# The spatial gate's second matrix in seven block products, with the fill share of VectorE raised from 0.85 to 0.88

## The chip, the cores and the metric

One NeuronCore of a Trainium2 chip runs the whole kernel. The metric is the device time of one execution in microseconds (us); lower is better.

## The reference, cut to what matters

One encoder layer over 512 positions of width 1024. A normalised input `xn` is projected to twelve column groups; four mixers work on them; each mixer's output is projected back, gated, and summed.

```python
xn = rms_norm(h, norm1_g[i])
proj = jnp.einsum('bsd,dk->bsk', xn, w_in[i])
(sg_u, sg_v, g_q, g_k, g_v, g_r, g_a, a_q, a_k, a_v, c_a, c_g) = jnp.split(proj, cuts, axis=-1)
y_a = spatial_gating(jax.nn.gelu(sg_u), jax.nn.gelu(sg_v), ...)   # u * (W_s layer_norm(v) + b)
...
for n, y in enumerate((y_a, y_b, y_c, y_d)):
    gate = jax.nn.sigmoid(jnp.einsum('bsd,de->bse', xn, w_gate[i, n]) + b_gate[i, n])
    merged = merged + gate * jnp.einsum('bsk,kd->bsd', y, w_branch[i, n])
```

`sg_u` is `xn` (512 x 1024) times a 1024 x 512 matrix. `y_d` is a causal depthwise convolution with 31 taps on 512 channels, followed by a layer norm.

## The kernel before, in words

**Three products for one.** Every fp32 factor is split into a high part (copied by ScalarE to a rounded type, `hi`) and a rest (VectorE: value minus `hi`, called `lo`). A product is hi*hi + hi*lo + lo*hi, so each 128-row block costs three matmuls on TensorE. The weights come from HBM in pieces of 128 x 1024 (512 KB): `load_piece` issues the transfer on SP's queue into a tile `raw` (four of them), `split_piece` makes `wh` and `wl` (five of each).

**Order of the work.** One Python loop writes the program: each `step` makes the weights of the next pieces ready (up to three pieces ahead), writes the matmuls, then `fill()`, then the step's own evacuation. Generators on a list `side` are advanced at the start and in the middle of a step and carry the small work of the mixers. Each engine executes its own instructions strictly in the order written.

**The taps.** The convolution's 31 x 4 multiply-adds (a tap: 128 x 512, VectorE, tiles `pad` and accumulators `u`) are a `filler`. `fill()` writes taps as long as the VectorE cost written so far is below `FILL` times the TensorE cost written so far; both are the kernel's own estimates. After the last tap `conv_norm` starts.

**The gates in seven products.** The gate matrices of mixers 1, 0 and 3 are done in halves (512 of 1024 columns; `(1, 0)` is the first half of mixer 1's). For each half, 2 x 2 blocks of input and weights are combined so that seven block products (`Q1` to `Q7`) do instead of eight. The sums of input blocks, `s1` to `s4`, are made once on VectorE (`combine`, and `last_sum` for `s4`, which overwrites a quarter of `xn` and so has to wait for the last product that reads the whole of `xn`). The sums of weight blocks are made by the transfers: a tile `grow` or `raw` gets one block by SP's queue and then one or more blocks by transfers that add, which only POOL's queue issues (`load_piece`, `accum_op`). `Q6` adds a block to the tile of `Q5`, and `Q4` one to that of `Q6`, so each of these transfers also waits for the split of the product before it.

**Around the change.** The order of this part is: mixer 2 with its gates (`branch(2)`), then `sg_v` in four pieces (four output banks at once; TensorE reads `lo` of a piece with its second matmul), then `sg_u` in four steps of 128 columns. Two of these stand ahead of the first half gate and two between its first products; the last one starts `sg_mix` (the 128 x 128 mixing on TensorE, then VectorE) and `last_sum`. For `sg_v` and for mixer 2's weights (`BY_DMA`) the rest `lo` is not made by VectorE: ScalarE writes minus `hi`, and an adding transfer on POOL's queue puts the weights on top. POOL's queue also computes the small powers for the norms.

Of the kernel before, what the change touches and what calls it, by code (L numbers as in the profile page):

```python
# [9 lines left out]
AF = mybir.ActivationFunctionType  # L10
# [3 lines left out]
S = 512  # L14
# [24 lines left out]
W_SLOTS = 5  # L39
LEAD = 3  # L40
RAW = 4
FILL = 0.85
WARM = 4
E_SLOTS = 26
PAD = 16
# [22 lines left out]

def gate_steps():

    out = []
    for i, e in enumerate(GATES + (None,)):
        for p in GATE_ORDER:
            if p in ("B0", "B1"):
                out.append((p, GATES[i - 1]) if i else ("S", 2 + int(p[1])))
            elif e is not None:
                out.append((p, e))
    return out


def layout():


    out = []
    loads = []
    at = {}

    def flush():
        for i in range(len(at.setdefault("done", [])), len(out)):
            at["done"].append(i)  # L90
            loads.append(((i,), out[i][-1], None))

    tok = lambda n: [("tok", "w_in", COL[n], 512, (2 * i, 2 * i + 1), 1024) for i in range(4)]
    ch = lambda n, m: ("ch", "w_in", COL[n] + 128 * m, 1024)
    out += tok("a_v")
    out += [("gka", i, 816 if i < 2 else 544) for i in range(3)]
    out += tok("g_v")
    for m in range(4):
        out += [ch("a_q", m), ch("a_k", m)]
    for m in range(4):  # L100
        out += [ch("c_g", m), ch("c_a", m)]
    out += [ch("g_q", m) for m in range(2)]
    out += [ch("g_r", m) for m in range(4)]

    def branch(n):
        for m in range(8):
            out.append(("gate", n, m, 1024))
            if m % 2 == 0:
                out.append(("br", n, m // 2, 1024))

    branch(2)
    out += tok("sg_v")
    out += [ch("sg_u", m) for m in range(2)]
    flush()
    last = {}
    blocks = {}
    for p, e in gate_steps():
        if p == "S":
            out.append(ch("sg_u", e))
            flush()  # L120
        elif p[0] == "B":
            if int(p[1]) % 2 == 0:
                out.append(("br", e[0], 2 * e[1] + int(p[1]) // 2, 1024))
                flush()
        else:
            if p == "Q5":
                for b in ("11", "12", "21", "22"):
                    blocks[b] = len(out)
                    out.append(("gblock", *e, int(b[0]) - 1, int(b[1]) - 1, 1024))
                    at["done"].append(blocks[b])  # L130
            old = GATE_ONTO.get(p)
            new = GATE_SUMS[p][len(GATE_SUMS[old]) if old else 0:]
            loads.append((tuple(blocks[b] for b in new), 1024, last[old] if old else None))
            last[p] = len(loads) - 1
    out += [("ch", "w_out", 128 * m, 1024) for m in range(8)]
    flush()
    ff1 = lambda g, m: ("ch", "w_ff1", 1024 * g + 128 * m, 1024)
    out += [ff1(0, m) for m in range(8)]
    flush()
    for g in range(4):  # L140
        blocks = {}
        for e in ("11", "12", "21", "22"):
            for h in range(2):
                blocks[e, h] = len(out)
                out.append(("ff2", g, int(e[0]) - 1, int(e[1]) - 1, h, 1024))
                at["done"].append(blocks[e, h])
        last = {}
        for e in ORDER if g < 3 else ORDER_LAST:
            if e[0] == "F":
                out.append(ff1(g + 1, int(e[1])))  # L150
                flush()
            elif e[0] == "U":
                out.append(("tok", "w_ple", 512 * int(e[1]), 512, (0, 1), 1024))
                flush()
            else:
                for h in range(2):
                    old = ONTO.get(e) if g < 3 or e != "Q5" else None
                    new = SUMS[e][len(SUMS[old]) if old else 0:]
                    loads.append((tuple(blocks[n, h] for n in new), 1024, last[old, h] if old else None))
                    last[e, h] = len(loads) - 1  # L160
    for half in range(2):
        out += [("tok", "w_ple_gate", 512 * half, 512, (2 * i, 2 * i + 1), 1024) for i in (2, 3, 0, 1)]
    flush()
    return out, loads
# [9 lines left out]
def build(tc, x, w, vec, wa2, sgw, rows, rb, pt, out):  # L174
# [17 lines left out]
    def U(dt=F32):  # L192
        return epool.tile([128, 512], dt, tag="u", bufs=E_SLOTS, name=name("u"))
# [153 lines left out]
    def start(g, wait=0, first=False):  # L347
        side.insert(0 if first else len(side), [g, wait, "start"])
# [125 lines left out]
    base = {}  # L474
    j = 0
    for key, n in (("a_v", 4), ("gka", 3), ("g_v", 4), ("qk", 8), ("conv", 8), ("g_q", 2), ("g_r", 4), ("br2", 12),
                   ("sg_v", 4), ("sg_u", 2)):
        base[key] = j
        j += n
    for p, e in gate_steps():  # L480
# [525 lines left out]
    def last_sum():  # L1006

        for f in range(4):
            copy(quarter(1, 0, 0, f), x4[f // 2][:, 256 * (f % 2):256 * (f % 2) + 256])
        yield "mid"  # L1010
        for f in range(4):
            tt(quarter(1, 0, 1, f), x4[f // 2][:, 256 * (f % 2):256 * (f % 2) + 256],
               quarter(1, 0, 0, f).bitcast(F32), OP.subtract)
        xsum["s4"] = [[quarter(1, 0, q, f) for q in range(2)] for f in range(4)]
# [49 lines left out]

    start(sg_bias(), 0)
    tok_steps("sg_v", 4, xn, 512, after)
    def sg_u(m, j):
        def evac(b):
            t = U()
            ACT.activation(t, b, AF.Gelu_apprx_tanh)  # L1070
            su.append(t)
            if m == 3:
                start(sg_mix(), 0)
                start(last_sum(), 0, True)

        step(j, lambda b: ch_mm(b, j, xn), evac)

    for m in range(2):
        sg_u(m, base["sg_u"] + m)
    for n, i, k in (("a11", 0, 0), ("a12", 0, 1), ("a22", 1, 1)):  # L1080
        xsum[n] = [[quarter(i, k, q, f) for q in range(2)] for f in range(4)]
    xr = []
# [14 lines left out]
    def gate_product(p, e):  # L1097
        j = base[p, e]
        n, u = e
        bk = {"Q1": 2, "Q6": 2, "Q7": 2, "Q4": 2, "Q5": 3, "Q3": 3, "Q2": 1}[p]  # L1100
        fresh = p in ("Q1", "Q2", "Q5")

        def mms(_):
            if fresh:
                gb[bk] = bank()
            b = gb[bk]
            xs = xsum[gsum[p]]
            hi, lo = parts[j]
            seq = [(hi, f, q, m) for f in range(4) for m in range(2) for q in range(2)]
            seq += [(lo, f, 0, m) for f in range(4) for m in range(2)]  # L1110
            for i, (t, f, q, m) in enumerate(seq):
                if i == len(seq) // 2:
                    middle()
                mm(b[:, 256 * m:256 * m + 256], t[:, 256 * f + 128 * m:256 * f + 128 * m + 128], xs[f][q],
                   fresh and i == 0, i == len(seq) - 1, skip_group_check=True)

        def evac(_):
            b = gb[bk]
            b2 = b.rearrange("p (m t) -> p m t", m=2)
            if p == "Q1":  # L1120
                ga[e] = mpool.tile([128, 2, 512], F32, tag="ga", bufs=2, name=name("ga"))
                copy(ga[e][:, :, 0:256], b2)
            elif p == "Q5":
                gc[e] = mpool.tile([128, 2, 512], F32, tag="gb", bufs=1, name=name("gb"))
                copy(gc[e][:, :, 256:512], b2)
            elif p == "Q6":
                copy(gc[e][:, :, 0:256], b2)
            elif p == "Q2":
                o = ga[e][:, :, 0:256]
                tt(o, o, b2, OP.add)  # L1130
                for m in range(2):
                    gate_tanh(o[:, m], o[:, m], n, 4 * u + m)
            elif p == "Q3":
                o = gc[e][:, :, 0:256]
                tt(o, b2, o, OP.subtract)
            elif p == "Q7":
                o = gc[e][:, :, 256:512]
                tt(o, o, b2, OP.subtract)
                for m in range(2):
                    gate_tanh(gc[e][:, m], gc[e][:, m], n, 4 * u + 2 + m)  # L1140
            elif p == "Q4":
                for m in range(2):
                    gate_tanh(ga[e][:, m, 256:512], b2[:, m], n, 4 * u + m)

        step(j, mms, evac, own=False)

# [7 lines left out]
             lambda b: merge(4 * u + m, th, b, last=n == 3))  # L1154

    for p, e in gate_steps():
        if p == "S":
            sg_u(e, base[p, e])
        elif p[0] == "B":
            branch_product(int(p[1]), e)  # L1160
            if p == "B3" and e == (0, 1):
                start(load_residual(), 4)
        else:
            gate_product(p, e)
# [449 lines left out]
```

## Time and profile before

| | |
|---|---|
| three timed runs | 986.45, 989.26, 989.85 us, median 989.26 |
| the profiled execution's own time | 988.05 us |
| its span, first to last instruction | 986.3 us |
| TensorE busy | 967.6 us, 98% of the span |
| VectorE, ScalarE, POOL busy | 684.9, 457.7, 98.5 us |
| TensorE's mean granted clock | 0.996 |

The profiled execution took 1.75 us more than its span. A row of a timeline gives the start of an instruction (or of several merged ones, with their count after x), how long it took, the engine, the source line, what it writes and reads, and in brackets the idle time of the engine ahead of it with what ended it. Matmuls overlap, so their spacing (from one row's start to the next row's) is their cost, not their length.

### The profile page before, as it was taken

To read this page: it belongs to the slowest core of one execution; us is meant where nothing else is said; L and a number is where in the kernel's file an instruction comes from. 1 tells how busy PE (TensorE), PEld (TensorE's weight loads), DVE (VectorE), ACT (ScalarE), POOL (GpSimd) and SP (SyncE) were. 2 spreads that over 40 slices of the span, in tenths; PEclk is the share of its full clock that TensorE was granted. 3 is DMA by queue.
4 is the path that set the end of the run, shared out by engine and by line. 5 is a ranking of instruction groups with operands and counts; after the bars stand their busy time and mean duration, and the time that the engine had idled before them with its cause. 6 is when DMAs were issued, how large, how long until landed. Compare 5 with 4: busy or idle time off the path is not lost.

```text
span 986.3 us, 12889 instructions
## 1 busy us (share of the span) xinstructions
PE 967.6 (98%) x4990; PEld 821.3 (83%) x4990; DVE 684.9 (69%) x993; ACT 457.7 (46%) x685; POOL 98.5 (10%) x119
## 2 busy tenths in 40 slices
PE   8999999999999999999999999999999999999995
PEld 6978888887888899998998888888888888887885
DVE  6645897477899887877666553566576577578656
ACT  6473774235363435455454334434343345335633
POOL 5001000002121201110110000010001002011000
PEclk9999999999999999999999999999999999999998
DMA  6344332247598538765974233366468267667402
GB/s 231 119 129 128 118 84 78 86 113 186 110 242 226 142 104 223 179 162 143 249 220 129 86 118 117 87 147 171 129 171 209 72 190 183 198 176 187 132 22 86
DMA packets 43225, 144.96 MB, mean 147 GB/s; under 512 B 4859, under 2 KB 5276, under 8 KB 43164
## 3 DMA queue, kind: packets, MB, share of 16 engines
q1 hardware_dynamic: 32156, 104.29, 31.4%
q0 software_dynamic: 11008, 39.85, 21.9%
q8 instruction: 39, 0.64, 0.3%
q14 instruction: 22, 0.18, 0.1%
HBM read 139.92 MB, written 2.10 MB: 144 GB/s over the span
## 4 chain that ended last, share of the span: by engine, by line
PE 87%; DVE 7%; ACT 3%; issue 2%; DMA 1%; POOL 0%; SPq 0%; POOLq 0%; ACTq 0%; DVEq 0%
PE b L236 85%; DVE wl L218 2%; PE b L240 2%; DVE u L218 1%; ACT wh L231 1%; DVE u L222 1%; DVE ht L218 1%; DMA raw<-w 0%; DMA stack<-stack 0%; ACT u L231 0%; DVE s L218 0%; DVE gb L218 0%; ACT combo L231 0%; DVE ga L222 0%; DVE ht L222 0%
## 5 line engine op out<-in xcount | busy, mean ns | idle before, releaser
L236 PE MATMUL b<-x,wh 128*128 128x512 f32 (+1 forms) x1440 | 315.6, 363 | 1.7 <-DVE gb L218 1.7
L236 PEld LDWEIGHTS b<-x,wh 128*128 128x128 f32 x1440 | 244.0, 189 | 43.4 <-issue 3.7
L218 DVE TENSOR_TENSOR wl<-raw,wh 128x1024 fp32r<-128x1024 f32 (+2 forms) x150 | 182.2, 1223 | 75.8 <-ACT wh L231 74.4
L231 ACT ACTIVATE wh<-raw 128x1024 fp32r<-128x1024 f32 (+2 forms) x166 | 169.5, 1039 | 27.3 <-DMA raw<-w 18.9
L236 PE MATMUL b<-x,wl 128*128 128x512 f32 (+1 forms) x720 | 168.2, 361 | 0.0
L236 PE MATMUL b<-wh,combo 128*128 128x512 f32 x448 | 141.7, 390 | 0.6 <-DVE ht L218 0.6
L236 PEld LDWEIGHTS b<-x,wl 128*128 128x128 f32 x720 | 123.9, 189 | 20.7
L236 PEld LDWEIGHTS b<-wh,combo 128*128 128x128 f32 x448 | 84.1, 188 | 18.4 <-issue 0.9
L1234 ACT ACTIVATE act<-act 128x512 f32<-128x512 f32 x32 | 20.2, 632 | 147.8 <-DVE act L222 147.8
L236 PE MATMUL b<-wl,combo 128*128 128x512 f32 x224 | 87.5, 391 | 0.9 <-DVE wl L218 0.9
L236 PE MATMUL b<-u,wh 128*128 128x512 f32 x320 | 84.2, 392 | 1.8 <-ACT u L231 1.6
L222 DVE SCALAR_TENSOR_TENSOR u<-pad,vecs,u 128x512 f32<-128x512 f32 x120 | 83.0, 745 | 0.0
L294 POOL DMA_DIRECT2D grow<-w x42 | 37.9, 951 | 359.7 <-DVE wl L218 297.5
L218 DVE TENSOR_TENSOR wl<-grow,wh 128x1024 fp32r<-128x1024 f32 x48 | 57.9, 1220 | 20.7 <-ACT wh L231 20.7
L236 PEld LDWEIGHTS b<-u,wh 128*128 128x128 f32 x320 | 59.2, 188 | 14.6 <-ACT u L231 1.9
L236 PE MATMUL b<-wh,x 128*128 128x512 f32 (+1 forms) x208 | 61.1, 374 | 0.0
L222 DVE SCALAR_TENSOR_TENSOR act<-b,v 128x512 f32<-128x512 f32 x32 | 22.0, 690 | 53.6 <-PE b L236 53.4
L236 PE MATMUL b<-wh,u 128*128 128x512 f32 (+1 forms) x192 | 54.9, 370 | 2.0 <-ACT wh L231 2.0
L231 ACT ACTIVATE wh<-grow 128x1024 fp32r<-128x1024 f32 x48 | 48.8, 1046 | 8.3 <-PE b L236 4.4
L236 PEld LDWEIGHTS b<-wl,combo 128*128 128x128 f32 x224 | 42.1, 188 | 10.6 <-DVE wl L218 2.1
L236 PE MATMUL b<-u,wl 128*128 128x512 f32 x160 | 46.7, 389 | 0.0
L236 PEld LDWEIGHTS b<-wh,x 128*128 128x128 f32 x208 | 38.1, 188 | 6.8
(196 smaller groups left out, 1178.7 us busy)
## 6 DMA issues: line engine op xcount, KB each, us to landing
raw<-w SPq DMA_DIRECT2D x161, 512.0 KB, 4.4
grow<-w POOLq DMA_DIRECT2D x42, 512.0 KB, 8.0
wl<-w POOLq DMA_DIRECT2D x16, 512.0 KB, 8.1
grow<-w SPq DMA_DIRECT2D x14, 512.0 KB, 5.2
raw<-w POOLq DMA_DIRECT2D x14, 512.0 KB, 7.5
h<-x SPq DMA_DIRECT2D x16, 256.0 KB, 7.1
v<-rb SPq DMA_DIRECT2D x8, 256.0 KB, 4.6
stack<-stack POOLq DMA_DIRECT2D x8, 256.0 KB, 4.2
```

The costliest lines, as they stand in the source:

```text
L218: return DVE.tensor_tensor(o, a, b, op=op)
L222: return DVE.scalar_tensor_tensor(o, a, s, b, op0=op0, op1=op1)
L231: return ACT.activation(o, a, AF.Copy, **k)
L236: PE.matmul(o, l, r, start=start, stop=stop, **k)
L240: PE.transpose(o, i, ident)
L294: POOL.dma_start(t[:, 0:n], w[i, :, 0:n], accum_op=OP.add)
L1234: ACT.activation(a, a, AF.Square)
```

## The change

`sg_u` becomes a half gate of its own kind, named `("u", 0)`: its 1024 x 512 matrix is loaded as four 512 x 256 blocks and done in seven block products. Six of them (`Q5 Q1 Q2 Q6 Q3 Q7`) stand ahead of the first gate half, the seventh (`Q4`) behind that half's `Q5` and `Q1`. `last_sum` starts after `sg_v`, `sg_mix` after the seventh product. `FILL` goes from 0.85 to 0.88.

```diff
-FILL = 0.85
+FILL = 0.88
 def gate_steps():
-    out = []
+    first = ("u", 0)
+    out = [(p, first) for p in "Q5 Q1 Q2 Q6 Q3 Q7".split()]
     for i, e in enumerate(GATES + (None,)):
         for p in GATE_ORDER:
             if p in ("B0", "B1"):
-                out.append((p, GATES[i - 1]) if i else ("S", 2 + int(p[1])))
+                if i:
+                    out.append((p, GATES[i - 1]))
+                elif p == "B1":
+                    out.append(("Q4", first))
...
-    def sg_u(m, j):
-        def evac(b):
-            t = U()
-            ACT.activation(t, b, AF.Gelu_apprx_tanh)
-            su.append(t)
-            if m == 3:
-                start(sg_mix(), 0)
-                start(last_sum(), 0, True)
-
-        step(j, lambda b: ch_mm(b, j, xn), evac)
+    start(last_sum(), 0, True)
...
             elif p == "Q4":
                 for m in range(2):
-                    gate_tanh(ga[e][:, m, 256:512], b2[:, m], n, 4 * u + m)
+                    if n == "u":
+                        ACT.activation(su[m][:, 256:512], b2[:, m], AF.Gelu_apprx_tanh)
+                    else:
+                        gate_tanh(ga[e][:, m, 256:512], b2[:, m], n, 4 * u + m)
+                if n == "u":
+                    start(sg_mix(), 0)
```

SP's queue before, where the loads of the last piece of `sg_v` (`raw_2660`) and of the steps behind it stand; `u` are rows and the mixing weights:

```order
L289 DMA raw_2660<-w 128x1024
L289 DMA raw_2720<-w 128x1024
L289 DMA raw_2727<-w 128x1024
L289 DMA grow_2789<-w 128x1024
L439 DMA u_2828<-rows 128x512
```

The same place of the change (`raw_2664` is the last piece of `sg_v`, `grow_2724` the tile of the first block product):

```order
L289 DMA raw_2664<-w 128x1024
L289 DMA grow_2724<-w 128x1024
L289 DMA raw_2732<-w 128x1024
L289 DMA raw_2794<-w 128x1024
L439 DMA u_2833<-rows 128x512
```

The growing tile has moved ahead of the two plain loads, directly behind the last load of `sg_v`.

POOL's queue before, from the `lo` of the first piece of `sg_v` (`wl_2716`) to that of the fourth (`wl_2854`):

```order
L308 DMA wl_2716<-w 128x1024
L308 DMA wl_2723<-w 128x1024
L308 DMA wl_2785<-w 128x1024
L294 DMA grow_2789<-w 128x1024
L1023 MEMSET u_2832 64x4x64
L308 DMA wl_2854<-w 128x1024
L294 DMA grow_2789<-w 128x1024
```

And of the change, where the pieces of `sg_v` are `wl_2720`, `wl_2728`, `wl_2790` and `wl_2859`:

```order
L308 DMA wl_2720<-w 128x1024
L294 DMA grow_2724<-w 128x1024
L308 DMA wl_2728<-w 128x1024
L308 DMA wl_2790<-w 128x1024
L1023 MEMSET u_2837 64x4x64
L308 DMA wl_2859<-w 128x1024
L294 DMA grow_2724<-w 128x1024
```

The adding transfer for the first block product now stands ahead of the `lo` of the second and third piece of `sg_v`.

VectorE before, from the first rows of `sg_mix` (`u_3293`) to the second split behind them; `u_1974` is a tap's accumulator, `ga` a half gate:

```order
L222 SCALAR_TENSOR_TENSOR u_3293<-b_3288,vecs,u_2830 128x512
L218 TENSOR_TENSOR u_3293<-u_3293,u_3039 128x512
L222 SCALAR_TENSOR_TENSOR u_3301<-b_3296,vecs,u_2830 128x512
L218 TENSOR_TENSOR u_3301<-u_3301,u_3085 128x512
L218 TENSOR_TENSOR wl_3324<-raw_3157,wh_3323 128x1024
L222 SCALAR_TENSOR_TENSOR u_1974<-pad_1869,vecs,u_1974 128x512
L218 TENSOR_TENSOR ga_3171<-ga_3171,b_3304 128x2x256
```

And in the change, from two steps ahead of the same place:

```order
L218 TENSOR_TENSOR wl_3329<-raw_3196,wh_3328 128x1024
L222 SCALAR_TENSOR_TENSOR u_1976<-pad_1936,vecs,u_1976 128x512
L218 TENSOR_TENSOR wl_3363<-raw_3227,wh_3362 128x1024
L222 SCALAR_TENSOR_TENSOR u_1970<-pad_1583,vecs,u_1970 128x512
L222 SCALAR_TENSOR_TENSOR u_1972<-pad_1762,vecs,u_1972 128x512
L222 SCALAR_TENSOR_TENSOR u_3388<-b_3383,vecs,u_2835 128x512
L218 TENSOR_TENSOR u_3388<-u_3388,u_3134 128x512
L222 SCALAR_TENSOR_TENSOR u_3396<-b_3391,vecs,u_2835 128x512
L218 TENSOR_TENSOR u_3396<-u_3396,u_3136 128x512
L218 TENSOR_TENSOR wl_3419<-raw_3265,wh_3418 128x1024
L222 SCALAR_TENSOR_TENSOR u_1974<-pad_1869,vecs,u_1974 128x512
L222 SCALAR_TENSOR_TENSOR u_1976<-pad_1936,vecs,u_1976 128x512
```

Behind the mixing two taps stand where one stood. The whole list has 4 taps more than before ahead of the split of the first step behind `sg_v`, 6 more ahead of that step's norm, and 3 fewer at the end of the first gate half; the last tap falls in the same product step.

## Rows read from the trace of the kernel before

**Rows 1.** Page, engines: busy us (share of the span) x instructions.

```profile
PE 967.6 (98%) x4990; PEld 821.3 (83%) x4990; DVE 684.9 (69%) x993; ACT 457.7 (46%) x685; POOL 98.5 (10%) x119
```

**Rows 2.** Page, chain that ended last: share of the span by engine.

```profile
PE 87%; DVE 7%; ACT 3%; issue 2%; DMA 1%; POOL 0%; SPq 0%; POOLq 0%; ACTq 0%; DVEq 0%
```

**Rows 3.** Timeline of TensorE, the second step of `sg_u` and two block products.

```profile
326.52 3.34 PE L236 MATMUL b<-x,wh 128*128 128x512 f32 x14
...
331.96 2.08 PE L236 MATMUL b<-s,wh 128*128 128x256 f32 x16
...
334.83 2.08 PE L236 MATMUL b<-x,wh 128*128 128x256 f32 x16
...
337.71 3.36 PE L236 MATMUL b<-x,wh 128*128 128x512 f32 x14
```

**Rows 4.** Windows: PE, PEld, DVE, ACT, POOL busy (x), PEclk, DMA share, GB/s.

```profile
282.00:286.00 4.00, 4.00 (x20) 3.30 (x19) 3.93 (x8) 3.64 (x4) 1.78 (x2) 1.00 1.07 277
...
327.00:352.00 25.00, 25.00 (x148) 22.25 (x147) 21.74 (x37) 10.53 (x17) 6.28 (x6) 1.00 0.65 169
...
376.00:407.00 31.00, 31.00 (x217) 29.08 (x217) 25.56 (x32) 13.97 (x19) 3.99 (x5) 1.00 0.72 193
```

**Rows 5.** Timeline of SP's queue, 281 to 287 us.

```profile
281.30 0.33 SPq L289 DMA_DIRECT2D raw<-w  x1
283.77 2.22 SPq L289 DMA_DIRECT2D raw<-w  x2
286.05 0.48 SPq L289 DMA_DIRECT2D grow<-w  x1
```

**Rows 6.** DMA issues on SP's queue at 281.3, 285.7, 286.0 us: us to landing.

```profile
raw<-w SPq DMA_DIRECT2D x1, 512.0 KB, 8.8
raw<-w SPq DMA_DIRECT2D x1, 512.0 KB, 11.9
grow<-w SPq DMA_DIRECT2D x1, 512.0 KB, 14.2
```

**Rows 7.** Timeline of POOL, the second piece of `sg_v` and the growing tile.

```profile
284.99 0.89 POOL L308 DMA_DIRECT2D wl<-w  x1 [0.79 <-ACT wl L231]
...
300.53 0.87 POOL L294 DMA_DIRECT2D grow<-w  x1 [4.74 <-DMA grow<-w]
```

**Rows 8.** DMA issues on POOL's queue at 275.2, 277.1, 300.5, 317.0 us.

```profile
wl<-w POOLq DMA_DIRECT2D x1, 512.0 KB, 7.0
wl<-w POOLq DMA_DIRECT2D x1, 512.0 KB, 8.9
grow<-w POOLq DMA_DIRECT2D x1, 512.0 KB, 8.2
grow<-w POOLq DMA_DIRECT2D x1, 512.0 KB, 5.5
```

**Rows 9.** Timeline of TensorE: first `lo` matmul of the second piece of `sg_v`.

```profile
304.08 0.39 PE L236 MATMUL b<-wl,x 128*128 128x512 f32 x1
```

**Rows 10.** Timelines of VectorE (six taps) and ScalarE (a wait for VectorE).

```profile
218.53 4.06 DVE L222 SCALAR_TENSOR_TENSOR u<-pad,vecs,u 128x512 f32<-128x512 f32 x6
...
272.76 0.63 ACT L231 ACTIVATE h<-u 128x512 fp32r<-128x512 f32 x1 [1.42 <-DVE u L222]
```

**Rows 11.** Timeline of VectorE from the last sum to the first half's Q4.

```profile
349.75 1.43 DVE L218 TENSOR_TENSOR x<-v,x 128x256 fp32r<-128x256 f32 x4 [0.26 <-ACT x L231]
351.62 1.22 DVE L218 TENSOR_TENSOR wl<-raw,wh 128x1024 fp32r<-128x1024 f32 x1 [0.44 <-ACT wh L231]
352.76 0.74 DVE L222 SCALAR_TENSOR_TENSOR u<-b,vecs,u 128x512 f32<-128x512 f32 x1
...
369.52 0.68 DVE L218 TENSOR_TENSOR gb<-gb,b 128x512 f32<-128x512 f32 x1
```

**Rows 12.** Timeline of TensorE: the first half gate's Q6 and Q4.

```profile
348.62 2.08 PE L236 MATMUL b<-s,wh 128*128 128x256 f32 x16
...
370.34 2.15 PE L236 MATMUL b<-x,wh 128*128 128x256 f32 x16 [1.02 <-DVE gb L218]
```

**Rows 13.** Page, group: line engine op out<-in xcount | busy us, mean ns | idle before.

```profile
L231 ACT ACTIVATE wh<-grow 128x1024 fp32r<-128x1024 f32 x48 | 48.8, 1046 | 8.3 <-PE b L236 4.4
```

More of the change, by code (lines that the diff above doesn't have):

```diff
@@ L112, in layout @@
     out += tok("sg_v")
-    out += [ch("sg_u", m) for m in range(2)]
     flush()
@@ L117, in layout @@
     for p, e in gate_steps():
[L118 to L121, printed above, removed]
+        if p[0] == "B":
             if int(p[1]) % 2 == 0:
@@ L127, in layout @@
                 for b in ("11", "12", "21", "22"):
-                    blocks[b] = len(out)
+                    blocks[e, b] = len(out)
                     out.append(("gblock", *e, int(b[0]) - 1, int(b[1]) - 1, 1024))
-                    at["done"].append(blocks[b])
+                    at["done"].append(blocks[e, b])
             old = GATE_ONTO.get(p)
             new = GATE_SUMS[p][len(GATE_SUMS[old]) if old else 0:]
-            loads.append((tuple(blocks[b] for b in new), 1024, last[old] if old else None))
-            last[p] = len(loads) - 1
+            loads.append((tuple(blocks[e, b] for b in new), 1024, last[e, old] if old else None))
+            last[e, p] = len(loads) - 1
     out += [("ch", "w_out", 128 * m, 1024) for m in range(8)]
@@ L476, in build @@
     for key, n in (("a_v", 4), ("gka", 3), ("g_v", 4), ("qk", 8), ("conv", 8), ("g_q", 2), ("g_r", 4), ("br2", 12),
-                   ("sg_v", 4), ("sg_u", 2)):
+                   ("sg_v", 4)):
         base[key] = j
@@ L1066, in build @@
     tok_steps("sg_v", 4, xn, 512, after)
-    def sg_u(m, j):
-        def evac(b):
-            t = U()
-            ACT.activation(t, b, AF.Gelu_apprx_tanh)
-            su.append(t)
-            if m == 3:
-                start(sg_mix(), 0)
-                start(last_sum(), 0, True)
-        step(j, lambda b: ch_mm(b, j, xn), evac)
-    for m in range(2):
-        sg_u(m, base["sg_u"] + m)
+    start(last_sum(), 0, True)
     for n, i, k in (("a11", 0, 0), ("a12", 0, 1), ("a22", 1, 1)):
@@ L1104, in mms @@
             if fresh:
-                gb[bk] = bank()
-            b = gb[bk]
+                gb[e, bk] = bank()
+            b = gb[e, bk]
             xs = xsum[gsum[p]]
@@ L1117, in evac @@
         def evac(_):
-            b = gb[bk]
+            b = gb[e, bk]
             b2 = b.rearrange("p (m t) -> p m t", m=2)
@@ L1131, in evac @@
                 for m in range(2):
-                    gate_tanh(o[:, m], o[:, m], n, 4 * u + m)
+                    if n == "u":
+                        su.append(U())
+                        ACT.activation(su[m][:, 0:256], o[:, m], AF.Gelu_apprx_tanh)
+                    else:
+                        gate_tanh(o[:, m], o[:, m], n, 4 * u + m)
             elif p == "Q3":
@@ L1139, in evac @@
                 for m in range(2):
-                    gate_tanh(gc[e][:, m], gc[e][:, m], n, 4 * u + 2 + m)
+                    if n == "u":
+                        su.append(U())
+                        ACT.activation(su[2 + m], gc[e][:, m], AF.Gelu_apprx_tanh)
+                    else:
+                        gate_tanh(gc[e][:, m], gc[e][:, m], n, 4 * u + 2 + m)
             elif p == "Q4":
                 for m in range(2):
-                    gate_tanh(ga[e][:, m, 256:512], b2[:, m], n, 4 * u + m)
+                    if n == "u":
+                        ACT.activation(su[m][:, 256:512], b2[:, m], AF.Gelu_apprx_tanh)
+                    else:
+                        gate_tanh(ga[e][:, m, 256:512], b2[:, m], n, 4 * u + m)
+                if n == "u":
+                    start(sg_mix(), 0)
         step(j, mms, evac, own=False)
@@ L1156, in build @@
     for p, e in gate_steps():
-        if p == "S":
-            sg_u(e, base[p, e])
-        elif p[0] == "B":
+        if p[0] == "B":
             branch_product(int(p[1]), e)
@@ L1577 @@
         elif e[0] == "gblock":
-            t = parts_first(a["w_gate"][0, e[1]][512 * e[3]:512 * e[3] + 512,
+            m, c = (w_in, COL["sg_u"]) if e[1] == "u" else (a["w_gate"][0, e[1]], 0)
+            t = parts_first(m[:, c:][512 * e[3]:512 * e[3] + 512,
                                                 512 * e[2] + 256 * e[4]:512 * e[2] + 256 * e[4] + 256])
```

## The prediction

> **What bounds the kernel now.** I read the page's engines first: TensorE is busy for 967.6 of 986.3 us, with VectorE at 69% and ScalarE at 46% [rows 1]. The chain that ended last agrees: 87% of it is TensorE, 7% VectorE [rows 2]. So a change pays by what it takes off TensorE's list, and loses by what it makes TensorE wait for. Then TensorE's timeline around the change. The reader should look at distances between starts: a step of `sg_u` takes 331.96 - 326.52 = 5.44 us and a block product 2.87 and 2.88 us [rows 3]. Last come the queues ahead of the place, because the block products get their weights through them.
>
> **The change part by part.**
>
> *TensorE's list.* Four steps of 5.44 us leave (21.8), seven products of 2.87 us come (20.1): **-1.7 us**. Weight loads are in these distances.
>
> *ScalarE and VectorE.* Three more pieces are split, at 1.22 us each on VectorE [rows 11], and three evacuations add a VectorE operation, 0.68 us as in the last row there: 5.7 us more. The stretch has VectorE at 21.7 of 25 us and ScalarE at 10.5 of 25 [rows 4], which would be too much for VectorE, but the taps give way: the fill rule writes 2 taps where the steps of `sg_u` had 13. I cost this at nothing here; what it costs later is the last item.
>
> *The earlier taps (0.88).* A tap is 4.06 / 6 = 0.68 us [rows 10]. TensorE does not read the taps, so the price is VectorE's lateness. Two taps more (some 1.3 us) stand ahead of the linear attention's last outputs, and ScalarE waits for those at 272.76 [rows 10] and then works on without a gap until it has released the load of `sg_v`'s last piece. So SP's issues around 281 us come 1.3 us later. Alone that costs TensorE nothing, as the weights of that stretch are ready ahead of need; it enters the next item.
>
> *The queues.* This is where I expect the first wait. In the change the first growing tile is issued directly behind the last load of `sg_v`: 281.30 + 0.33 [rows 5], plus 1.3 for the later ScalarE, is 283.0 us. The transfers are saturated there (share 1.07 [rows 4]). SP's loads issued at 281.3, 285.7 and 286.05 landed after 8.8, 11.9 and 14.2 us [rows 5, 6], so at 290.1, 297.6 and 300.3: the load between the first two must have landed near 293.8, and one landing follows another after some 3.7 us. The growing tile takes that place, so it lands at 293.8 + 1.3 = 295.1. POOL waits for that landing before it can issue the adding transfer (as it did at 300.53, after 4.74 us idle [rows 7]), and in the change `lo` of `sg_v`'s second piece is queued behind it; before, that went out at 284.99 [rows 7]. An adding transfer issued at 295.2 into an empty POOL queue beside SP's loads takes 7.0 us, and one issued 1.9 us after such a one landed 3.8 us behind it (275.2 + 7.0 = 282.2; 277.1 + 8.9 = 286.0 [rows 8]). That gives 302.2 and 306.0. TensorE reads this `lo` at 304.08 [rows 9]: a wait of 1.9 us; I take **+1.7**, since SP has by then loaded for three microseconds alone. Bounds: nothing, if both transfers went as fast as the one at 317.0 (5.5 us [rows 8]: 302.6 for the second); 3.1 us with 8.2 us for the first [rows 8] (295.2 + 8.2 + 3.8 = 307.2). The third piece's `lo` follows 3.8 us later at 309.8, and is read 24 matmuls and the bias product later, past 310.3: no second wait.
>
> The Trainium skill ("DMA: Bandwidth & Descriptors", Anatomy of one DMA, SWDGE path) fits one such transfer as 2.0 us plus bytes over 436 GB/s, which would be about 3.2 us for 512 KB, an estimate from that page; the rows show 5.5 us at the quietest. By the page `lo` would land near 300 us and the sum would be without the 1.7.
>
> *The seven products themselves.* They run from the end of `sg_v`. POOL's queue is free of loads long before the norms' powers. Most splits come several microseconds ahead; the closest point is `Q7`, whose bank is released by ScalarE's copy of `Q6` after `Q2`'s addition and GELU. I count some 0.5 us of slack and cost it at nothing; without that cover it is under 1 us.
>
> *The first gate half.* Before, TensorE came to its `Q4` at 369.3 and waited 1.02 us for VectorE's last `gb` operation, which ended at 370.2 [rows 11, 12]. VectorE is late there because the mixing starts at 352.76, 4.14 us after `Q6` (348.62), and the chain from it to that operation takes 17.4 us. In the change the four `s4` sums (1.43 us [rows 11]) have left this stretch, but the withheld taps come back: six of them and four splits stand between the split of this half's `Q6` and the mixing (6 x 0.68 + 4 x 1.14 = 8.6 us, a split taking 352.76 - 351.62 = 1.14), and two taps behind it instead of one. That first split waits for an adding transfer which POOL can issue only after the split of `Q5`. Following the order with these durations I find that issue some 11.5 us ahead of `Q6`'s matmuls; 6 to 7 us for the transfer (between 5.5 and 7.0 [rows 8]) and 1.05 us for ScalarE's copy [rows 13] put the split 3 to 4 us ahead of them. Mixing then starts 4.5 to 5.5 us after `Q6`, and the last `gb` operation ends 17.4 + 0.7 us later, 22.6 to 23.6 us after `Q6`, while TensorE arrives after 20.7 (369.32 - 348.62). The wait grows from 1.0 to 1.9 or more: **+1.0** (bounds: -1.0, if the wait goes because the `s4` work left; +2.7, if that transfer takes 8.2 for 5.5 us).
>
> *Behind it.* The convolution's norm moves by a step against the gates and its work stays the same; I take 0, bounds -0.7 and +0.7, from the size of the waits that it meets there now.
>
> **Sum.** -1.7 + 1.7 + 1.0 = **+1.0 us**. Against the profiled execution's 988.05 that is 989.05. The three timed runs and the profiled one have a mean of 988.4 and lie within 3.4 us of each other, so I add to that mean: **989.4 us**. With 0.5% of 989.26, or 4.9 us, as what a measurement can tell from no change, this is no change.
>
> **Rivals.**
>
> *A, the waits are hidden and the list pays.* POOL's transfers land ahead of 304.1, and the first half's wait goes with the `s4` work: -1.7 - 1.0 = -2.7, so 985.7 us. For it: transfers issued into a quiet queue took 5.5 us, and 1.4 us of VectorE's work, with ScalarE's copies for it, really leaves the first half. Against it: share 1.07 just ahead of the place, and the eight taps that come back. The skill's fit above is this rival's case for its first half; the trace's durations do not bear it out.
>
> *B, slower: the growing tile holds up POOL's queue.* If its base takes the 14.2 us that the growing tile took before [rows 6] instead of 12, it lands at 297.2, and issued 0.2 later and with 8.2 and 3.8 us behind it `lo` comes at 309.4: a wait of 5.3 us, in all -1.7 + 5.3 + 1.0 = +4.6, so 993.0. It decides from the point where the base lands after some 296 us. For it: the same kind of transfer, in the same saturated stretch. Against: it is third in SP's queue where the other was fifth.
>
> *C, the change doesn't do what it says*: products starve for weights, since nine transfers serve 20 us of work. A half gate takes eleven in 31 us, at a share of 0.72 [rows 4], and 9/20 against 11/31 is a quarter more, so below 1. I give it no case of its own beyond the rest.
>
> **How the numbers follow.** Forecast 0.45, A 0.33, B 0.15, anything else 0.07. The range reaches over A and into B: A's 985.7 less the 1.7 us half-spread of the runs gives 984.0; the forecast with all its upper bounds is -1.7 + 3.1 + 2.7 + 0.7 = +4.8, or 993.2, about where B lies too, and with half of that scatter 994.0. More than 0.5% faster (under 984.3) needs A and a fast set of runs, or a gain that I don't see: 0.10. More than 0.5% slower (over 994.2) needs B and more: 0.10. The rest, 0.80, is within 0.5%.
>
> **What would show it.** Distances of 2.87 us between seven products behind `sg_v`; a TensorE wait of 1 to 2 us for a POOL transfer at about 304 us, with POOL idle until the growing tile has landed near 295; a wait for `gb` of about 2 us at the first half's `Q4`; the last tap near 412 us. No wait at 304 and none at that `Q4` would be A. Waits inside the seven products, or a wait at `sg_v`'s third or fourth piece, would make the prediction wrong in its steps.

## The result and the profile after

The change makes the kernel slower: 996.57 us (median of 994.56, 996.13, 997.00 and 997.59) against 989.22 us of the kernel before on the same chip. The ratio is 1.0078, with a 95% interval from 1.0066 to 1.0090. The profiled execution took 994.56 us with a span of 992.8 us, 6.5 us more than that of before. It is the fastest of the four: the others are 1.6 to 3.0 us longer, at a mean granted clock of 0.992 to 0.994 for its 0.995, and what they lost beyond it does not stand in the rows below. The forecast was no change, at 989.4 us.

The page first: busy us by engine and the chain that ended last.

```profile
PE 967.9 (97%) x5062; PEld 824.0 (83%) x5062; DVE 690.3 (70%) x999; ACT 462.4 (47%) x693; POOL 101.9 (10%) x123
...
PE 76%; DVE 9%; issue 6%; ACT 4%; DMA 2%; POOL 1%; SPq 0%; POOLq 0%; ACTq 0%; DVEq 0%
```

TensorE is busy for as long as before [rows 1], though its list is 1.6 us shorter (below), so the 6.5 us are waits, and time at a lower clock. Its share of the chain has fallen from 87% [rows 2] to 76%, which says that the chain now leaves TensorE more often; 11% of the span is far more than 6.5 us, so the share does not measure the loss. Where the 6.5 us are is read off TensorE's timeline, by the start of the same instruction in both kernels. First the rows of the kernel before that the prediction had not needed (columns as in the rows above):

```profile
273.93 3.34 PE L236 MATMUL b<-x,wh 128*128 128x512 f32 x14
277.10 1.75 PE L236 MATMUL b<-x,wl 128*128 128x512 f32 x7
...
434.34 0.60 PE L240 MATMUL b<-ident,s 128*128 128x128 f32 x4
...
437.65 2.08 PE L236 MATMUL b<-s,wh 128*128 128x256 f32 x16
...
467.14 2.15 PE L236 MATMUL b<-x,wh 128*128 128x256 f32 x16 [0.69 <-DVE gb L218]
...
541.78 0.50 PE L236 MATMUL b<-u,wh 128*128 128x512 f32 x1 [1.55 <-ACT u L231]
```

And TensorE in the change:

```profile
273.64 3.33 PE L236 MATMUL b<-x,wh 128*128 128x512 f32 x14
277.29 1.88 PE L236 MATMUL b<-x,wl 128*128 128x512 f32 x7 [0.31 <-DMA wl<-w]
...
303.26 0.62 PE L236 MATMUL b<-wh,x 128*128 128x512 f32 x2
303.71 0.39 PE L236 MATMUL b<-wl,x 128*128 128x512 f32 x1
...
306.99 0.50 PE L236 MATMUL b<-wl,x 128*128 128x512 f32 x1 [2.43 <-DMA wl<-w]
...
308.21 1.05 PE L236 MATMUL b<-wh,x 128*128 128x512 f32 x2
309.06 0.63 PE L236 MATMUL b<-wl,x 128*128 128x512 f32 x1
...
325.74 2.08 PE L236 MATMUL b<-s,wh 128*128 128x256 f32 x16
...
328.61 2.08 PE L236 MATMUL b<-x,wh 128*128 128x256 f32 x16
...
351.65 2.08 PE L236 MATMUL b<-s,wh 128*128 128x256 f32 x16
...
374.20 2.14 PE L236 MATMUL b<-x,wh 128*128 128x256 f32 x16 [1.84 <-DVE gb L218]
...
442.22 0.65 PE L240 MATMUL b<-ident,s 128*128 128x128 f32 x4 [0.97 <-POOL s L421]
442.63 2.15 PE L236 MATMUL b<-s,wh 128*128 128x256 f32 x16
...
473.15 2.15 PE L236 MATMUL b<-x,wh 128*128 128x256 f32 x16 [1.67 <-DVE gb L218]
...
547.78 0.50 PE L236 MATMUL b<-u,wh 128*128 128x512 f32 x1 [1.54 <-ACT u L231]
```

| instruction | before | after | difference | what the step adds |
|---|---|---|---|---|
| last gate of mixer 2, `wh` | 273.93 | 273.64 | -0.3 | start of the execution |
| the same gate, `wl` | 277.10 | 277.29 | +0.2 | +0.5: a wait for `lo` from POOL's queue |
| second piece of `sg_v`, first `lo` [rows 9] | 304.08 | 306.99 | +2.9 | +2.7: the wait of 2.43 |
| end of `sg_v` (before: 326.52 - 5.44 [rows 3]) | 321.08 | 325.74 | +4.7 | +1.8: half clock |
| first half's `Q6` [rows 12] | 348.62 | 351.65 | +3.0 | -1.6: the shorter list |
| first half's `Q4` [rows 12] | 370.34 | 374.20 | +3.9 | +0.8: a longer wait for `gb` |
| `Q5` behind the conv norm's transposes | 437.65 | 442.63 | +5.0 | +1.1: a wait for POOL |
| `Q4` of half (0, 1) | 467.14 | 473.15 | +6.0 | +1.0: a longer wait for `gb` |
| first `w_out` step, its last input | 541.78 | 547.78 | +6.0 | nothing |

The difference is still 6.0 us in TensorE's rows at 900 us; the last 0.5 of the 6.5 us lies behind them and was not traced.

The clock in the rows: the two matmuls of the row at 308.21 take 0.85 us to the next row, where the two at 303.26, ahead of the wait, took 0.45. The windows (PE, PEld, DVE, ACT and POOL busy, then PEclk, DMA share, GB/s) show the granted clock falling after the wait, part of each window at 1.2 for 2.4 GHz:

```profile
300.00:305.00 5.00, 4.56 (x21) 3.43 (x19) 4.93 (x10) 1.65 (x2) 1.17 (x2) 1.00 1.05 256
305.00:310.00 5.00, 3.01 (x9) 2.39 (x10) 4.97 (x9) 0.47 (x1) 0.86 (x1) 0.78 1.06 272
310.00:315.00 5.00, 5.00 (x25) 4.21 (x24) 1.32 (x3) 0.80 (x1) 1.50 (x2) 0.88 1.06 252
```

Five us at 0.78 and five at 0.88 of full speed are 1.1 + 0.6 = 1.7 us lost, the table's fourth step. In the kernel before the clock is 1.00 in every window of ten us from 20 to 970 us.

POOL and SP in the change show the cause of the wait as it was foretold:

```profile
282.77 0.42 SPq L289 DMA_DIRECT2D grow<-w  x1
```

```profile
284.35 0.89 POOL L308 DMA_DIRECT2D wl<-w  x1 [1.81 <-ACT wl L231]
295.59 0.88 POOL L294 DMA_DIRECT2D grow<-w  x1 [10.35 <-DMA grow<-w]
296.13 2.12 POOL L308 DMA_DIRECT2D wl<-w  x2
```

POOL stands for 10.35 us until the growing tile's base has landed; `lo` of the second piece goes out behind it, and lands just ahead of 306.99.

### The profile page after: what moved, and what is told of

It reads as the page before. It is cut to its first block, busy times and chain, and to the rows that moved or that the text cites. A ratio compares the mean times of both kernels' runs of the same rounds, so it can differ in the third digit from the quotient of the medians.

```text
span 992.8 us, 13057 instructions
## 1 busy us (share of the span) xinstructions
PE 967.9 (97%) x5062; PEld 824.0 (83%) x5062; DVE 690.3 (70%) x999; ACT 462.4 (47%) x693; POOL 101.9 (10%) x123
## 4 chain that ended last, share of the span: by engine, by line
PE 76%; DVE 9%; issue 6%; ACT 4%; DMA 2%; POOL 1%; SPq 0%; POOLq 0%; ACTq 0%; DVEq 0%
PE b L236 75%; DVE u L222 2%; DVE wl L218 2%; PE b L240 2%; ACT wh L231 2%; DVE u L218 2%; DMA wl<-w 1%; DVE ht L218 1%; DMA stack<-stack 1%; POOL s L421 0%; DVE s L218 0%; ACT u L231 0%; ACT wl L231 0%; DMA raw<-w 0%; DVE gb L218 0%
## 5 line engine op out<-in xcount | busy, mean ns | idle before, releaser
L236 PE MATMUL b<-x,wh 128*128 128x512 f32 (+1 forms) x1440 | 307.6, 358 | 3.5 <-DVE gb L218 3.5
L236 PEld LDWEIGHTS b<-x,wh 128*128 128x128 f32 x1440 | 240.0, 189 | 42.4 <-issue 5.0
L236 PE MATMUL b<-x,wl 128*128 128x512 f32 (+1 forms) x720 | 164.3, 356 | 0.3 <-DMA wl<-w 0.3
L236 PEld LDWEIGHTS b<-x,wl 128*128 128x128 f32 x720 | 121.9, 189 | 20.2 <-DMA wl<-w 0.7
L218 DVE TENSOR_TENSOR wl<-grow,wh 128x1024 fp32r<-128x1024 f32 x51 | 61.6, 1221 | 24.4 <-ACT wh L231 24.4
L294 POOL DMA_DIRECT2D grow<-w x45 | 41.1, 966 | 363.7 <-DVE wl L218 281.5
L231 ACT ACTIVATE wh<-grow 128x1024 fp32r<-128x1024 f32 x51 | 52.1, 1047 | 8.2 <-DMA grow<-w 8.1
```

The source lines that it names most:

```text
L218: return DVE.tensor_tensor(o, a, b, op=op)
L231: return ACT.activation(o, a, AF.Copy, **k)
L236: PE.matmul(o, l, r, start=start, stop=stop, **k)
L294: POOL.dma_start(t[:, 0:n], w[i, :, 0:n], accum_op=OP.add)
```

## The experiments

All medians are device times; the ratio is to the kernel before, run on the same chip in between. Its median was 988.0 to 989.2 us on the chips used, so a difference of medians between rows is good to about 1 us.

| kernel | median us | ratio (95%) |
|---|---|---|
| the change | 996.57 | 1.0078 (1.0066 to 1.0090) |
| fill88: before, fill share 0.88 | 997.15 | 1.0095 (1.0081 to 1.0109) |
| blocks85: change, fill share 0.85 | 995.25 | 1.0077 (1.0063 to 1.0090) |
| defer88: change, queue order repaired | 994.11 | 1.0066 (1.0053 to 1.0079) |
| defer85: the same, fill share 0.85 | 991.59 | 1.0034 (1.0021 to 1.0046) |
| shift4: defer88, four taps moved ahead | 992.04 | 1.0037 (1.0025 to 1.0050) |
| shift4s: shift4, transposes a product later | 992.34 | 1.0034 (1.0020 to 1.0047) |
| shift_q: change, four taps moved ahead | 995.84 | 1.0075 (1.0063 to 1.0088) |
| after885: change, fill share 0.885 | 998.27 | 1.0093 (1.0078 to 1.0108) |
| shift885: shift4, fill share 0.885 | 990.26 | 1.0016 (1.0007 to 1.0025) |
| hold885: shift885, no taps in the mixing | 988.35 | 1.0001 (0.9989 to 1.0013) |
| ramp885: hold885, fill share from 0.86 up | 987.71 | 0.9997 (0.9987 to 1.0006) |
| rampq885: ramp885, the change's queue order | 992.97 | 1.0055 (1.0039 to 1.0071) |

**Each part alone (fill88, blocks85).** The edits are `FILL = 0.88` in the kernel before, and `FILL = 0.85` in the change.

> The kernel before with the fill share 0.88 alone. Theory (the loss is mostly the queue's: about 2.8 us of waiting at the second piece of sg_v and about 2 us of half clock behind it): the earlier taps alone cost little, a wait of 0.3 us at mixer 2's gate near 277 us and whatever the later conv norm meets; 989 to 991.5 us, no wait near 304 us. Rival F (the fill share is the change that costs): 994 to 997 us, with the larger gb waits and the wait for POOL at the norm's transposes in it.

> The block products with the fill share left at 0.85. Theory: the queue order is the same as in the change, so the wait at the second piece of sg_v stays, shorter by the some 1.3 us by which SP's loads go out earlier (1 to 2.4 us), with the half clock behind it; 991 to 995 us. Rival F: the loss goes with the fill share, no wait near 305 us, 986 to 988.5 us. Rival G (the fill share is innocent, the blocks cost all): 996 to 997 us.

The fill share alone costs 9.2 us and the block products alone 7.3 us, yet both together cost 7.4: they are not two terms of a sum. What couples them, as I read the rows, is the place of the conv norm. Its first matmul (with `mean`) starts at 421.35 us in the kernel before, at 428.07 in the change, but at 398.22 in fill88 and 450.57 in blocks85. Block products put more VectorE work into the fill rule's ledger, so at 0.85 the taps end a half gate later; at 0.88 without that work they end most of a half earlier. fill88 then waits where the early norm meets the gates, with the clock behind each wait: 0.75 and 0.91 in the two windows of five us from 405 us on, and the window below (timeline of TensorE; then its window, columns as above):

```profile
406.86 1.33 PE L236 MATMUL b<-ones,u 128*128 128x1 f32 x8 [1.98 <-DVE u L218]
...
442.63 3.75 PE L236 MATMUL b<-x,wh 128*128 128x256 f32 x16 [4.45 <-DVE gb L218]
```

```profile
442.00:449.00 7.00, 6.37 (x32) 6.40 (x33) 5.79 (x9) 4.10 (x7) 0.86 (x1) 0.54 0.66 150
```

So both of my theories for these two were too simple: the small cost for fill88 was wrong by some 6 us, and the wait expected near 277 us is not there. Rival F's number for fill88 was met (within 0.2 us), but its claim that the loss goes with the fill share is wrong for blocks85, and so is rival G's, that the share is innocent. blocks85 lies at the edge of what I expected; it has the queue's wait and, at the late norm's other end, a second wait where `w_out` begins (the kernel before has one of 1.55 us there, blocks85 has two). Its profiled execution, 991.09 us at a clock of 0.996, is 4 us faster than its other four (995.01 to 995.79 us, clock 0.991), so these rows show the waits but not all of the time lost:

```profile
303.21 0.50 PE L236 MATMUL b<-wl,x 128*128 128x512 f32 x1 [2.10 <-DMA wl<-w]
...
539.94 0.51 PE L236 MATMUL b<-u,wh 128*128 128x512 f32 x1 [1.48 <-ACT u L231]
...
542.71 0.50 PE L236 MATMUL b<-u,wh 128*128 128x512 f32 x1 [1.55 <-ACT u L231]
```

**The queue's order repaired (defer88, defer85).** The adding transfer of the first growing tile is kept and issued behind `sg_v`'s third `lo`:

```diff
+            if j == FIRST_GROWN:
+                held_adds.append(add)
...
+        if j == FIRST_GROWN - 2:
+            while held_adds:
+                held_adds.pop(0)()
```

> The change with one edit: the adding transfer of the first growing tile is issued behind the lo transfers of sg_v's second and third piece, as in the kernel before. Theory: the wait near 305 us and the half clock behind it go, 4.5 to 5 us, so 991.5 to 992.5 us; the larger gb waits and the wait for POOL stay. Rival (it is bandwidth, not the queue's order: the landing is as late when it is issued earlier): 995 to 997 us, the wait stays over 1.5 us. Second rival: the first block product then waits for its growing tile, 993 to 995 us, with a wait near 321 us.

> The same edit and the fill share 0.85: the block products without the queue wait and without the earlier taps. Theory: the list's gain of 1.7 to 2 us is left, less a gb wait of up to 1 us: 986.5 to 989 us. Rival F (fill alone matters): the same as the block products with 0.85 and without the edit. Rival G (the blocks cost something else too): 990 us or more.

The wait at 305 us is gone from both, so it was the queue's order and not the bandwidth. But defer88 gains little on the change, 0.1% by the ratios, whose intervals overlap, and 2.5 us by the medians, not 4.5 to 5; its 994.11 us missed the 991.5 to 992.5 expected. The reason is a wait that the queue had hidden (VectorE, then TensorE of defer88, whose line numbers are one or more higher):

```profile
345.54 1.23 DVE L219 TENSOR_TENSOR wl<-grow,wh 128x1024 fp32r<-128x1024 f32 x1 [3.98 <-ACT wh L232]
...
354.07 0.74 DVE L223 SCALAR_TENSOR_TENSOR u<-b,vecs,u 128x512 f32<-128x512 f32 x1
```

```profile
336.25 2.18 PE L237 MATMUL b<-s,wh 128*128 128x256 f32 x16 [0.75 <-ACT gb L232]
...
347.87 2.08 PE L237 MATMUL b<-s,wh 128*128 128x256 f32 x16
...
372.32 3.55 PE L237 MATMUL b<-x,wh 128*128 128x256 f32 x16 [3.74 <-DVE gb L219]
```

VectorE stands 3.98 us for the weights of the first half's `Q6`, six taps and three splits queue behind that split, and the mixing starts 354.07 - 347.87 = 6.2 us after `Q6`. In the change the late TensorE gave VectorE time to catch up: there the mixing starts 4.3 us after `Q6`. defer85 missed its 986.5 to 989 us: it begins `w_out` 1.3 us earlier than the kernel before (536.41 for 537.72), meets the same two waits there as blocks85 (1.47 and 1.55 us, at 539.86 and 542.62), and has half clock behind them (0.70 and 0.62 in the two windows of five us from 540 us on). Its norm is as late as that of blocks85 (450.49 us); that the late norm makes the second wait was not tested by a run of its own.

**The taps ahead of the first half's Q6 (shift4, shift_q, shift4s).** Four taps are written ahead of that half's `Q5`, in shift4 on top of defer88, in shift_q on the change as it is; shift4s also has `yield 2` for `yield 1` ahead of the norm's transposes.

```diff
+            if (p, e) == ("Q5", (1, 0)):
+                force(4)
             gate_product(p, e)
```

> The change with the first adding transfer behind sg_v's lo transfers (as defer88) and one more edit: four taps are written right ahead of the step of the first half gate's Q5, so that VectorE has them to do while it waits for the weights of that half's Q6 (it was idle there for 3.98 us in defer88, with six taps queued behind). Theory (Q4 of the first half waits because the mixing is queued behind those taps): the mixing starts 2.7 us earlier, the wait for gb there goes from 3.74 to about 1 us and the half clock behind it goes, so 4 us less than defer88: 989.5 to 991 us. Rival (the mixing is late for another reason, such as the weights of Q6 themselves or ScalarE): the wait stays over 3 us, 993.5 to 995 us.

> The change with the four taps moved ahead of the first half gate's Q5, and the queue left as the change has it. Theory: the wait at sg_v's second piece (2.4 us) and what the clock loses behind it stay, the wait for gb at the first half's Q4 goes from 1.84 us to nothing, since VectorE had 2.56 us of idle time there: 1.5 to 2 us less than the change, 994.5 to 995.2 us. Rival (the taps are not what is late): no difference to the change, 996 to 997 us.

> shift4 with the conv norm's transposes on TensorE one product later. Theory: the 0.97 us that TensorE waited for POOL at them goes, 0.5 to 1 us less than shift4. Rival (the norm's VectorE work behind them then comes later too and meets the third mixer's products): the same as shift4 or up to 1.5 us more, with the wait at the second later Q4 over 1.7 us.

In shift4 the wait falls from 3.74 to 1.84 us and not to 1, and the median of 992.04 us missed the 989.5 to 991 expected; in shift_q the wait does not move at all, since VectorE, with the taps done, stands 1.72 us for ScalarE's copy of the last weights ahead of the mixing. The theory held for what the queued taps did to defer88, and was wrong on what is left: TensorE and VectorE of shift4 show a floor.

```profile
348.19 2.08 PE L237 MATMUL b<-s,wh 128*128 128x256 f32 x16
...
351.07 1.95 PE L237 MATMUL b<-u,u 128*128 128x128 f32 x16
...
370.74 2.74 PE L237 MATMUL b<-x,wh 128*128 128x256 f32 x16 [1.84 <-DVE gb L219]
```

```profile
352.49 0.75 DVE L223 SCALAR_TENSOR_TENSOR u<-b,vecs,u 128x512 f32<-128x512 f32 x1
...
358.14 1.41 DVE L223 SCALAR_TENSOR_TENSOR u<-pad,vecs,u 128x512 f32<-128x512 f32 x2
...
369.91 0.68 DVE L219 TENSOR_TENSOR gb<-gb,b 128x512 f32<-128x512 f32 x1
```

The mixing now starts 1.4 us after the start of its own matmuls (1.3 us in the kernel before), 4.3 us after `Q6`, so there is little left to gain ahead of it; from its start to that of the last `gb` operation it is 17.4 us, two taps included, against 16.8 with one tap [rows 11]. In shift4s the wait for POOL is gone (no wait at its transposes at 440.99), but its median is that of shift4: its timed runs lie between 988.3 and 994.1 us, the two fastest at a mean granted clock of 0.996, the two slowest at 0.991. Its profiled execution also ran at 0.84 and 0.82 in the two windows of five us from 5 us on, ahead of anything that the edit touches. Whether the repair pays by itself stays inconclusive there.

**The conv norm's place (after885, shift885).** The edit is `FILL = 0.885`, in the change and in shift4.

> The change with the fill share at 0.885 for 0.88, which puts the conv norm's matmuls on TensorE back to the place among the gate's products where they stand in the kernel before (one product earlier than in the change). Theory (the wait for POOL at the norm's transposes and the larger wait for gb at the second later Q4 come from that place): the first goes (0.97 us), the second falls from 1.67 to 0.7, so some 2 us less than the change, 994 to 995 us. Rival (they come from VectorE being full, wherever the norm stands): the waits stay or grow, 996 us or more.

> The same place of the conv norm, with the queue's and the taps' repairs of shift4. Theory: 2 us less than shift4: 989.5 to 990.5 us, with the wait of 1.84 us at the first half's Q4 left. Rival: the same as shift4, 991.5 us or more.

```profile
308.76 0.57 PE L236 MATMUL b<-wl,x 128*128 128x512 f32 x1 [3.93 <-DMA wl<-w]
...
377.82 2.47 PE L236 MATMUL b<-x,wh 128*128 128x256 f32 x10 [3.70 <-DVE gb L218]
...
443.08 0.60 PE L240 MATMUL b<-ident,s 128*128 128x128 f32 x4
...
475.91 2.15 PE L236 MATMUL b<-x,wh 128*128 128x256 f32 x16 [0.69 <-DVE gb L218]
```

These rows of after885 show both sides. The transposes wait for nothing, and the wait of 1.67 us is back at the 0.69 of the kernel before: the place of the norm made these two waits. But the higher share writes one tap more ahead of the weights of `sg_v`, ScalarE and SP are later by about 1 us, the queue's wait grows from 2.43 to 3.93 us, and the wait for `gb` at the first half's `Q4` from 1.84 to 3.70 us, so the time does not fall; the expected 994 to 995 us were missed on that side. (Its profiled execution lost some 1.7 us more to the clock between 5 and 15 us, as that of shift4s did.) With the queue repaired (shift885) it is 1.8 us faster than shift4 by the medians, near the 2 that were expected.

**No taps inside the mixing chain (hold885), a later rise of the share (ramp885), and the queue alone (rampq885).**

```diff
     def fill():
+        if nofill[0]:
+            return
-        while filler and cost["dve"] < FILL * cost["pe"]:
+        while filler and cost["dve"] < share[0] * cost["pe"]:
...
+            share[0] = min(FILL, share[0] + 0.005)
+            if (p, e) in (("Q6", (1, 0)), ("Q5", (1, 1))):
+                nofill[0] = p == "Q6"
```

`FILL` is 0.885 in all three. The lines with `share` are those of ramp885 and rampq885, where it starts at 0.86 and rises by 0.005 with each product.

> shift885 without any taps written between the first half's Q6 and its Q4 (they follow behind it). Theory (the mixing chain from its first VectorE row to the last gb row takes 17.4 us with one tap in it, so each tap in it is 0.67 us of TensorE's wait there): with the two taps gone, the wait at that Q4 falls from 1.84 to about 0.5 us; 988 to 989.5 us. Rival (the taps written behind it make the next half late): a new wait for gb or ga in the next half, 990 us or more.

> hold885 with the fill share at 0.86 up to the first block product and rising to 0.885 over the next five steps, so that five taps fewer stand ahead of sg_v and the rest of the order is the same. Theory (the earlier taps make ScalarE late and with it the weights of mixer 2's last gate): the wait at 277 us (0.35 us, 0.6 us of TensorE's time against the kernel before) goes, 0.5 us less than hold885: 987 to 988 us, 0.5 to 1 us faster than the kernel before. Rival (that wait is noise of one execution): the same as hold885 and as the kernel before.

> ramp885 with POOL's queue as in the change, the growing tile's adding transfer ahead of sg_v's lo transfers: the price of that order alone, with all other repairs in. Theory: a wait of 2 to 2.5 us at the second piece of sg_v and the half clock behind it, of which nothing is hidden later, 3 to 5 us more than ramp885: 990.5 to 992.5 us. Rival (the later waits take back what the queue costs): up to 1.5 us more than ramp885.

In hold885 the wait at that `Q4` is 0.19 us (0.5 expected), no wait takes its place in the next half, and the kernel is level with the one before. ramp885 has no wait at 277 us, as expected, but is not measurably faster than hold885 or the kernel before. With these repairs the block products are worth nothing that this measurement can tell; what they would be worth without any wait of their own is not shown, since the profiled execution of ramp885 (the slowest of its twelve) still waits 0.66 us at `Q7` and 1.64 us for ScalarE at 459 us, where hold885 waits 0.49. rampq885 puts a price on the queue's order alone: 5.3 us more than ramp885, a little over the 3 to 5 expected, with the wait and the clock of the change back (timeline of TensorE, windows as above):

```profile
306.46 0.79 PE L236 MATMUL b<-wl,x 128*128 128x512 f32 x1 [2.61 <-DMA wl<-w]
```

```profile
305.00:310.00 5.00, 3.54 (x9) 2.83 (x10) 4.87 (x8) 0.00 (x0) 1.73 (x2) 0.66 1.06 279
```

Five us at 0.66 are 1.7 lost to the clock; 2.6 + 1.7 = 4.3 of the 5.3 us. The same execution lost another 1.7 us (0.66 in the five us from 545) behind the wait at `w_out`, where that of ramp885 lost nothing. Over all runs the mean granted clock is 0.993 in rampq885 and 0.9956 in ramp885, which on 990 us is, as an estimate, 2.6 us more lost to the clock; with the wait of 2.6 that makes 5.2.

## Why the prediction was wrong, point by point

Two steps failed: the queues' term, +1.7, which had no part for the clock behind the wait and measured 4.5, and *Behind it*, taken as 0, which measured 2.1. With 0.5 us at 277 us these misses make 5.4 us; the table's +6.0 and the forecast's +1.0 differ by 5.0.

*TensorE's list, -1.7:* right. Between the end of `sg_v` and the first half's `Q6` the change gains 1.6 us, and the products stand 2.87 us apart.

*The queues, +1.7:* the mechanism was right row by row: growing tile issued at 282.77 (283.0 foretold), its adding transfer at 295.59 (295.2), `lo` there at about 306.9 (306.0). The step that failed is the size, "I take +1.7". The wait was 2.43 us, still inside the bounds: `lo` landed 0.9 us later than foretold and TensorE came 0.5 us later. And no term had the clock. After the wait TensorE ran at half clock for a while and lost another 1.7 us. The term measured 4.5 in the table, and 5.3 in the pair ramp885 and rampq885. The Trainium skill ("TensorE: Matmul & The Clock Gate", HAM oscillation) describes a kernel that is set back to the low clock by its waits for transfers, and counts half of the time spent there as lost. These rows agree on the price (0.85 us for two matmuls that had taken 0.45), but the waits that it speaks of are longer than the 2.43 us here. The fit of the Trainium skill for one such transfer ("DMA: Bandwidth & Descriptors", Anatomy of one DMA, SWDGE path) gives 3.2 us for 512 KB, an estimate from that page. It is not borne out: the growing tile's adding transfer took 7.5 us here.

*The earlier taps, "alone that costs TensorE nothing":* right for the taps alone, and wrong by 0.5 us, the wait at 277 us, in the change. In fill88 the first `lo` of that gate goes out 6.7 us ahead of its matmul, as in the change (8.0 us in the kernel before), lands after 6.5 us, and nothing waits. In the change the same transfer took 7.1 us (7.1 to 7.2 in four others with block products), and TensorE stands; why it takes longer is not traced. With a fill share of 0.86 up to there the wait is gone (ramp885).

*The seven products, nothing:* right in the change, and the closest point was the one named: with TensorE earlier (defer88), `Q7` waits 0.75 us for ScalarE's copy, the price given for the case without cover.

*The first half's Q4, +1.0:* measured +0.8. The mixing started 4.3 us after `Q6`, a little under the 4.5 to 5.5 foretold, and the second tap lengthened the chain as foretold. But it came out right by luck, for two reasons. The prediction's own rows give a wait of 1.9 to 2.9 us, so +0.9 to +1.9, and it took the low end; and the queue's wait helped: without that (defer88) the wait is 3.74 us, 2.7 more than before, which is the term's upper bound. Rival A, the hidden waits, could not have given its 985.7 us.

*Behind it, 0 with bounds of 0.7:* this step failed. It took the norm's work as unchanged and asked only for the waits that it meets now; a shift of one product made one new wait and one longer one, 2.1 us in all. POOL of the kernel before, then VectorE and POOL of the change, at the transposes:

```profile
430.74 1.37 POOL L421 TENSOR_TENSOR s<-s,mhalf 128x4 f32<-128x4 f32 x1
```

```profile
438.42 1.23 DVE L218 TENSOR_TENSOR wl<-raw,wh 128x1024 fp32r<-128x1024 f32 x1 [2.35 <-ACT wh L231]
...
440.28 0.69 DVE L218 TENSOR_TENSOR u<-u,gb 128x512 f32<-128x512 f32 x1
440.89 0.15 DVE L228 TENSOR_SCALAR s<-b 128x4 f32<-128x4 f32 x1
```

```profile
441.13 1.04 POOL L421 TENSOR_TENSOR s<-s,mhalf 128x4 f32<-128x4 f32 x1 [4.50 <-DVE s L228]
```

The norm's sums end on TensorE near 435.5 us, but the 0.15 us operation that reads them now stands behind a split, which itself waits 2.35 us for ScalarE's copy, and two rows of a merge on VectorE, so POOL's power starts 5.6 us after the sums, where in the kernel before it started 1.8 us after them (428.9 and 430.74), and the transposes wait. That the place did it, and not a full VectorE, is what after885 showed; VectorE is idle in those 2.35 us.

*The sum:* -0.3 + 0.5 + 2.7 + 1.8 - 1.6 + 0.8 + 1.1 + 1.0 = +6.0 by the table, where I had +1.0. Rival B's number was nearest (+4.6), but by luck, with a different cause inside: the base landed near 295.5 and not 297.2, and the clock and the norm made up its 5.3 us of waiting.

## What to carry to other kernels

Price a wait of the engine that bounds the kernel together with the clock behind it: here one of 2.4 us cost 1.7 us more, one of 4.5 us 3.2 more, and one of 2.1 us, in one execution, nothing. When a filler's rule keeps a ledger of estimated costs, any work added or removed moves everything that follows the filler; look first where that follower lands. And a wait can hide another: after repairing one, read the same timeline again, since defer88 gave 2 to 3 of the 4.5 us that it had won back, most of it to a wait 65 us later.

## What the runs showed of the hardware that I had not expected

Waits of 1.5 to 4.5 us of TensorE were followed by stretches at half clock in some executions and not in others: 2.43 us in the change were (0.78 and 0.88 of full speed in the two windows), 2.10 us at the same place in the profiled execution of blocks85 were not (1.00 from 303 to 311 us). The 1.55 us at `w_out` that every kernel has cost the kernel before nothing, and shift885, in its profiled execution, a clock of 0.91 and 0.75 in the two windows of five us from 540 us on. After 4.45 us in fill88 the loss was larger, 0.46 of seven us, 3.2 us. Runs of one kernel spread by as much, and their mean granted clock with them, as in shift4s above, so one profiled execution can hold a loss, or lack one, that the median has not.
